# Recurrent gates as three products of high and low parts, low parts prepared early, and a tile's steps joined, in a two-layer hybrid flow step on one core

## The chip, the cores and the metric

The kernel runs on one core of one Trainium2 chip. The metric is device microseconds (us) of one execution. The time of the kernel before is 1498.38 us, the median of 3 runs (1497.87 to 1498.54). Engines are named as in the profile: PE is TensorE's products, PEld its weight loads, DVE VectorE, ACT ScalarE, POOL GpSimd and SP SyncE, which issues transfers.

## The reference

Two layers on 640 tokens (512 latents, 128 context) of width 1024, all in float32. Layer 0 mixes tokens by neighbourhood attention, layer 1 by a bidirectional gated linear recurrent unit; each is followed by a SwiGLU feed-forward. Every sub-layer has a norm, a shift and scale computed from the conditioning vector ("modulations"), and a gated residual. What the change touches is the recurrent unit:

```
xc  = depthwise conv of width 4 (xm @ w_x)             # 1024 channels, 8 blocks of 128
r   = sigmoid(xc_block @ w_a_block + b_a)              # per direction
i   = sigmoid(xc_block @ w_i_block + b_i)              # per direction
a   = exp(-8 * r * softplus(-lam))
b   = sqrt(1 - a^2) * (i * xc)
h_t = a_t * h_(t-1) + b_t                              # forward and backward
y   = gelu(xm @ w_g) * (h_forward + h_backward)        # then y @ w_lo
```

## The kernel before

Activations lie transposed: 128 channels of a tile in the partitions, tokens along the free axis. A dense weight is cut into units of 128 output channels by 1024 input channels (512 KB). A unit is used as a high part in TensorE's faster f32 format (`whi`, type fp32r) and a low part, what the high part leaves of the full value (`wlo`). The activations are split in the same way (`big` high and low). A product of full accuracy is three products: high by high, high by low, low by high (L239 to L241). `unit` (L170 to L189) prepares a unit: the raw weight comes by an SP transfer, the high part by ACT or by a POOL transfer that casts on the way, and DVE subtracts one from the other for the low part (L188).

The work goes through one program order that a scheduler fills in; each engine's instructions run in the order in which they stand on it, and so do the transfers of each queue. The stages, by the profiled execution:

- attention, to about 311 us;
- the first feed-forward with the attention's output projection ("ffn0", to about 835 us): 22 inner tiles in three chunks, each tile with a gate and an up unit (`ws`), then the chunk's down projection. Beside it DVE computes the remaining modulations: each step of the generator `mods` loads a 512 KB piece (`mraw`) on POOL's queue and multiplies it with the conditioning vector (`mprod`, L263 to L269). `fill(n)` takes n steps at each weight unit, up to a quota of the phase;
- the recurrent stage (835 to 1003 us): 8 tiles f of 128 channels. For each tile there are two weight units: `lru_xr` (the input of the conv) and `lru_gate` (the gelu branch). Each has 24 products of 384 columns and 24 of 256. `lru_a` does the conv on DVE and ACT and then the gate products: 2 gates by 2 directions, 643 columns (512 latents, 3 zeros and 128 context tokens) in plain f32 with one 128 by 128 weight block each, as products of 512 and 131 columns (L1407). ACT takes their tanh from PSUM (`gp`, two buffers, L1408). `lru_b` makes the coefficients (two exponential curves, a root) on ACT and DVE, with activation table loads (L1386) between the kinds of curve; `lru_c` the scans and the sum of both directions on DVE; `lru_d` and `lru_end` the product with the gelu branch and the split into `yhi`, `ylo`. The loop runs KT + 2 = 10 rounds: round t does `lru_a` of tile t, the input unit of tile t + 1, `lru_b` of tile t - 1, and `lru_c`, the gelu unit and `lru_d` of tile t - 2;
- the projection `project_halves` with w_lo (from about 980 us): 75 products over the first five input tiles of five outputs, then the later tiles as they become ready (L1093, L1097);
- the second feed-forward, to 1495 us, of which nothing is changed.

Of the kernel before, what the change touches and what calls it, by code (L numbers as in the profile page):

```python
# [15 lines left out]
P = 128  # L16
D = 1024
# [16 lines left out]
VW = 256  # L34
LW = 643
NLT = 10
C0 = 515
LATPR = (slice(0, 512), slice(C0, LW))
FG = (1, 1, 1)
MODS = ((0, 2), (0, 4), (0, 3), (0, 5), (1, 1), (1, 0), (1, 4), (1, 3), (1, 2), (1, 5))  # L40
# [87 lines left out]
class _Step:  # L128
# [40 lines left out]

    def unit(self, src, slot=None, after=None, nx=3, cast=False, raw=None):  # L170
        nc = self.nc
        _, a, b = src.shape
        raw = self.raw(src) if raw is None else raw
        if slot is None:
            self.nu += 1
            slot = "x" if self.wx and self.nu % 2 == 0 else "m"
        if slot == "x":
            hi, lo = self.wxs([P, a, b], nx)
        else:
            hi = self.t([P, a, b], F32R, "whi", 3)  # L180
            lo = self.t([P, a, b], F32R, "wlo", 3)
        if cast or self.ptags == ["at"]:
            with self.pin(self.cast if after else None):
                nc.gpsimd.dma_start(hi, src)
        else:
            nc.scalar.copy(hi, raw)  # L186
        with self.pin(after):
            self.low = nc.vector.tensor_tensor(lo, raw, hi.bitcast(F32), ALU.subtract).ins  # L188
        return hi, lo  # L189
# [70 lines left out]
    def mod_cols(self, l, j, out):  # L260
        nc = self.nc
        for f in range(KT):
            w = self.t([P, D], F32, "mraw", 2, self.sb)  # L263
            nc.gpsimd.dma_start(w, self.i["wm"][l * 6 + j - 2, f])  # L264
            for s in range(2):
                prod = self.t([P, D], F32, "mprod", 1, self.sb)
                with self.tc.issue_after(self.anchor) if self.anchor else nullcontext():
                    nc.vector.scalar_tensor_tensor(prod, w, 1.0, self.csb[:, s], ALU.mult, ALU.mult, accum_out=out[:, s, f:f + 1])  # L268
            yield  # L269
        nc.vector.tensor_tensor(out, out, self.col(f"bm{l}{j}").unsqueeze(1).broadcast_to([P, 2, KT]), ALU.add)  # L270
# [15 lines left out]
    def modulations(self):  # L286
        yield from self.mod_gate(0, 2)
        yield from self.mod_ss(0, 3, 1)
        yield from self.mod_gate(0, 5)
        yield from self.mod_ss(1, 0, 0)  # L290
        yield from self.mod_ss(1, 3, 1)
        yield from self.mod_gate(1, 2)
        yield from self.mod_gate(1, 5)

    def fill(self, n):
# [698 lines left out]
    def ffn(self, l, hi, lo, fp, last):  # L994
        nc = self.nc
        f0 = 0
        for ci, n in enumerate((8, 7, 7)):
# [23 lines left out]
            for j in range(n):  # L1021
                f = f0 + j
                self.ws(self.i["gu"][l, f], hi, lo, eg(j), FG[0] * (f > 0), CHB)
                self.ws(self.i["gu"][l, NF + f], hi, lo, eu(j), FG[1] * (f > 0), CHB)
            w = self.i["dn"][l, :, :, f0:f0 + n]
            if ci == 2:
                last(w, hhi, hlo, (l, 5))
            else:
                self.project(w, hhi, hlo, (l, 5), done=lambda f: self.fill(FG[2]))
            f0 += n  # L1030
# [334 lines left out]

    def halves(self, w, hi, lo, ev, after=None, slot=None):
        u = self.unit(w, slot, after, 2)
        return [lambda t0=t0, t1=t1, **kw: ev(t0, self.chunk(u, hi, lo, t0, t1, **kw)) for t0, t1 in CHL]

    def lru_xr(self, f, hi, lo, after=None):  # L1370
        xr = self.xrs[f % 2]
        nat = xr[:, 2:514].rearrange("p (r c) -> p c r", r=ROWS)

        def ev(t0, ps):
            for o, a, b, r in ((nat[:, 56:64], 0, 64, ROWS), (nat[:, 0:40], 64, 384, ROWS),
                               (nat[:, 40:56], 384, 512, ROWS), (xr[:, 517:645], 512, 640, 0)):
# [3 lines left out]
        return self.halves(self.i["wi"][KT + f], hi, lo, ev, after)  # L1380

# [8 lines left out]
    def lru_a(self, f, lp):  # L1390
        nc, xr = self.nc, self.xrs[f % 2]
        gw = self.t([P, 2, 2, P], F32, "gw", 2, lp)
        nc.sync.dma_start(gw, self.i["wg"][f])
        xc = self.t([P, LW], F32, "xc", 2, lp)
        nc.scalar.activation(xc, xr[:, 0:LW], AF.Identity, scale=self.col("cw0", f), bias=self.col("cb", f))
        for j in range(1, 4):
            nc.vector.scalar_tensor_tensor(xc, xr[:, j:j + LW], self.col(f"cw{j}", f), xc, ALU.mult, ALU.add)

        def lt():
            return self.t([P, 2, LW], F32, "lt", NLT, lp)  # L1400
        tr, ti = lt(), lt()
        for w, tl in enumerate((tr, ti)):
            for d in range(2):
                c = (w * 2 + d) * KT + f
                ps = self.pp.tile([P, 1024], F32, tag="gp", name=self.nm("gp"), bufs=2)
                for s0, s1 in ((0, 512), (512, LW)):
                    nc.tensor.matmul(ps[:, s0:s1], gw[:, w, d], xc[:, s0:s1], start=True, stop=True)  # L1407
                self.turn(AF.Exp, lambda: nc.scalar.activation(tl[:, d], ps[:, 0:LW], AF.Tanh, scale=0.5, bias=self.hb[:, c:c + 1]))  # L1408
        nc.vector.scalar_tensor_tensor(ti, ti, 1.0, xc[:, None, :].broadcast_to([P, 2, LW]), ALU.add, ALU.mult)
# [29 lines left out]
    def states(self, f, h):  # L1439
        ends = bass.AP(tensor=h.tensor, offset=h[:, 0, LW - 1:LW].offset, ap=[list(h.ap[0]), [C0 + 1, 2]])  # L1440
        return self.nc.vector.tensor_copy(self.st.rearrange("p (d k) -> p k d", d=2)[:, f], ends)

    def lru_c(self, f, a, h):
# [5 lines left out]
        for piece in ((56, 64, 0), (0, 56, 64)):  # L1449
            self.directions(y, h, *piece)  # L1450
        self.nc.vector.tensor_tensor(y[:, NLAT:NTOK], h[:, 0, C0:LW], h[:, 1, C0:LW], ALU.add)
        return y
# [12 lines left out]
    def lru_end(self, f, a, h, root, G, yhi, ylo, late):  # L1465
# [30 lines left out]
        dve(self.directions, y, h, 32, 56, 320)  # L1496
        dve(nc.vector.tensor_tensor, y[:, NLAT:NTOK], h[:, 0, C0:LW], h[:, 1, C0:LW], ALU.add)
        gated(*CH[1])
# [11 lines left out]
    def lru_gate(self, f, hi, lo, lp, after=None):  # L1510
# [3 lines left out]
        def ev(t0, ps):  # L1514
# [4 lines left out]
            for v, o in ((G, G),) if f == KT - 1 else ((ps, G[:, t0:NTOK]), (G[:, 0:t0], G[:, 0:t0])):  # L1519
                self.turn(AF.Gelu_apprx_tanh, lambda: nc.scalar.activation(o, v, AF.Gelu_apprx_tanh))  # L1520
        return G, self.halves(self.i["wi"][f], hi, lo, ev, after)

# [8 lines left out]
    def run(self):  # L1531
# [13 lines left out]
        self.cs = self.t([P, 2 * KT], F32, "cs", 1)  # L1545
        dram = self.ctx.enter_context(tc.tile_pool(name="dram", bufs=1, space=bass.MemoryType.DRAM))
        mpool, xpool = ExitStack(), ExitStack()
# [14 lines left out]
        V = V.rearrange("p k t -> p (k t)")[:, 0:NT * D].rearrange("p (t d) -> p t d", t=NT)  # L1562
        O = self.big(F32)
        with self.phase("attn", tp=2, sp=2, op=1, quota=24) as ap:
            self.kz = [self.t([P, 2, 960], F32R, f"KZ{j}", 1, ap) for j in range(2)]
# [32 lines left out]
        xd = dram.tile([D, NTOK], F32, tag="xd", name="xd")  # L1598
        with self.phase("ffn0", at=2, rr=1, mx=2, wx=2, quota=56) as fp:
# [5 lines left out]
            self.ffn(0, xhi, xlo, fp, last)  # L1605
        xpool.close()
        mpool.close()
# [5 lines left out]
        with self.phase("lru", at=1) as lp:  # L1613
            A, B, C, G = {}, {}, {}, {}
            self.table, self.last_act = AF.Gelu_apprx_tanh, None
# [66 lines left out]
```

## Time and profile before

| what | us |
|---|---|
| median of 3 runs | 1498.38 (1497.87 to 1498.54) |
| the profiled execution | 1496.74 |
| its span, from the first to the last instruction | 1494.9 |
| PE busy | 1475.9 (99%) |
| DVE busy | 1062.0 (71%) |
| ACT busy | 698.6 (47%) |
| POOL busy | 225.7 (15%) |
| granted TensorE clock, mean | 0.998 |

The profile is one execution on the hardware. A timeline row gives start, duration, engine, line, operation, the buffers written and read, the shape and the count; in square brackets the idle time of the engine just before, and what ended it. A row of a group gives busy time, the mean in ns of one instruction, and the idle time before them with what ended it. A transfer's row gives its queue, count, size and the median time from issue to landing. Successive products overlap on TensorE, so the duration of a product is longer than the distance to the next start.

### The profile page before, as it was taken

To read this page: it belongs to the slowest core of one execution; us is meant where nothing else is said; L and a number is where in the kernel's file an instruction comes from. 1 tells how busy PE (TensorE), PEld (TensorE's weight loads), DVE (VectorE), ACT (ScalarE), POOL (GpSimd) and SP (SyncE) were. 2 spreads that over 40 slices of the span, in tenths; PEclk is the share of its full clock that TensorE was granted. 3 is DMA by queue.
4 is the path that set the end of the run, shared out by engine and by line. 5 is a ranking of instruction groups with operands and counts; after the bars stand their busy time and mean duration, and the time that the engine had idled before them with its cause. 6 is when DMAs were issued, how large, how long until landed. Compare 5 with 4: busy or idle time off the path is not lost. (4 is left out here: it accounts for less than half of the span.)

```text
span 1494.9 us, 26171 instructions
## 1 busy us (share of the span) xinstructions
PE 1475.9 (99%) x10399; PEld 1433.0 (96%) x10399; DVE 1062.0 (71%) x2019; ACT 698.6 (47%) x1269; POOL 225.7 (15%) x264
## 2 busy tenths in 40 slices
PE   9999999999999999999999999999999999999997
PEld 7999999899999999999999988899999999999997
DVE  5778998679999987444443769886975666655645
ACT  5676667754332123312321569875634343424243
POOL 0212132101111110000000100000331322232311
PEclk9999999999999999999999999999999999999999
DMA  9645665345566664222222444335333131313111
GB/s 378 201 128 177 196 189 163 105 156 183 196 187 195 207 197 142 63 85 85 66 62 96 142 145 126 115 115 194 102 130 98 57 114 57 113 57 111 59 57 71
DMA packets 73050, 198.88 MB, mean 133 GB/s; under 512 B 8128, under 2 KB 24672, under 8 KB 72800
## 3 DMA queue, kind: packets, MB, share of 16 engines
q1 hardware_dynamic: 57360, 142.31, 29.9%
q0 software_dynamic: 14960, 54.21, 11.8%
q8 instruction: 82, 1.34, 0.4%
q10 hardware_dynamic: 608, 0.69, 0.1%
q14 instruction: 40, 0.33, 0.1%
HBM read 181.05 MB, written 8.92 MB: 127 GB/s over the span
## 5 line engine op out<-in xcount | busy, mean ns | idle before, releaser
L240 PE MATMUL mm<-big,whi 128*128 128x320 f32 (+3 forms) x1193 | 371.2, 311 | 0.8 <-DVE big L1508 0.6
L239 PE MATMUL mm<-big,whi 128*128 128x320 f32 (+3 forms) x1193 | 369.0, 311 | 1.6 <-ACT big L615 0.6
L241 PE MATMUL mm<-big,wlo 128*128 128x320 f32 (+3 forms) x1193 | 368.8, 310 | 0.0
L239 PEld LDWEIGHTS mm<-big,whi 128*128 128x128 f32 x1193 | 223.9, 188 | 3.7 <-ACT big L615 0.9
L240 PEld LDWEIGHTS mm<-big,whi 128*128 128x128 f32 x1193 | 224.2, 188 | 2.8 <-DVE big L1508 1.0
L241 PEld LDWEIGHTS mm<-big,wlo 128*128 128x128 f32 x1193 | 224.7, 188 | 1.1
L268 DVE SCALAR_TENSOR_TENSOR mprod<-mraw,csb 128x1024 f32<-128x1024 f32 x160 | 194.8, 1218 | 11.3 <-DMA mraw<-in_wm 10.8
L639 DVE SCALAR_TENSOR_TENSOR x<-mm,G,x 128x128 f32<-128x128 f32 (+3 forms) x193 | 77.4, 433 | 78.5 <-PE mm L241 77.0
L186 ACT CAST whi<-raw 128x1024 fp32r<-128x1024 f32 (+1 forms) x70 | 72.8, 1040 | 106.1 <-PE mm L240 71.2
L188 DVE TENSOR_TENSOR wlo<-raw,whi 128x1024 fp32r<-128x1024 f32 (+1 forms) x87 | 105.1, 1208 | 23.9 <-ACT whi L186 11.0
L240 PE MATMUL mm<-big,whx 128*128 128x320 f32 (+3 forms) x363 | 112.2, 309 | 0.0
L241 PE MATMUL mm<-big,wlx 128*128 128x320 f32 (+3 forms) x363 | 112.1, 309 | 0.0
L239 PE MATMUL mm<-big,whx 128*128 128x320 f32 (+3 forms) x363 | 111.9, 308 | 0.0
L264 POOL DMA_DIRECT2D mraw<-in_wm x80 | 43.4, 543 | 355.5 <-DVE mprod L268 257.3
L240 PE MATMUL mx<-big,whi 128*128 128x320 f32 (+3 forms) x299 | 92.1, 308 | 0.0
L239 PE MATMUL mx<-big,whi 128*128 128x320 f32 (+3 forms) x299 | 91.9, 307 | 0.0
L241 PE MATMUL mx<-big,wlo 128*128 128x320 f32 (+3 forms) x299 | 91.8, 307 | 0.0
L186 ACT CAST whx<-raw 128x1024 fp32r<-128x1024 f32 (+1 forms) x38 | 39.1, 1028 | 94.1 <-PE mm L240 54.5
L1506 ACT CAST whi<-raw 128x1024 fp32r<-128x1024 f32 (+1 forms) x41 | 41.3, 1007 | 69.0 <-PE mm L240 43.0
L240 PE MATMUL mx<-big,whx 128*128 128x320 f32 (+3 forms) x234 | 72.9, 312 | 0.0
L241 PE MATMUL mx<-big,wlx 128*128 128x320 f32 (+3 forms) x234 | 72.6, 310 | 0.0
L239 PE MATMUL mx<-big,whx 128*128 128x320 f32 (+3 forms) x234 | 72.4, 309 | 0.0
(409 smaller groups left out, 3734.3 us busy)
## 6 DMA issues: line engine op xcount, KB each, us to landing
raw<-in_gu SPq DMA_DIRECT2D x88, 512.0 KB, 3.5
mraw<-in_wm POOLq DMA_DIRECT2D x80, 512.0 KB, 3.9
raw<-in_dn SPq DMA_DIRECT2D x24, 512.0 KB, 3.6
sw<-in_wm SPq DMA_DIRECT2D x16, 512.0 KB, 10.2
raw<-in_wqk SPq DMA_DIRECT2D x16, 512.0 KB, 4.9
raw<-in_wi SPq DMA_DIRECT2D x16, 512.0 KB, 3.5
whi<-in_wi POOLq DMA_DIRECT2D x16, 512.0 KB, 3.8
raw<-in_dn SPq DMA_DIRECT2D x16, 448.0 KB, 3.3
```

Of the source, the lines that this page charges most:

```text
L186: nc.scalar.copy(hi, raw)
L188: self.low = nc.vector.tensor_tensor(lo, raw, hi.bitcast(F32), ALU.subtract).ins
L239: nc.tensor.matmul(ps, hi[:, k], xhi[:, k, s], start=(k == 0), stop=False)
L240: nc.tensor.matmul(ps, hi[:, k], xlo[:, k, s], start=False, stop=False)
L241: self.done = nc.tensor.matmul(ps, lo[:, k], xhi[:, k, s], start=False, stop=(k == last)).ins
L264: nc.gpsimd.dma_start(w, self.i["wm"][l * 6 + j - 2, f])
L268: nc.vector.scalar_tensor_tensor(prod, w, 1.0, self.csb[:, s], ALU.mult, ALU.mult, accum_out=out[:, s, f:f + 1])
L639: self.added = self.nc.vector.scalar_tensor_tensor(xs, ps[:, a - t0:b - t0], G[:, s, f:f + 1], xs, ALU.mult, ALU.add).ins
L1506: self.nc.scalar.copy(hi, v)
```

## The change

Three things are changed together.

1. The gate products. The row of 643 columns is made 644 long (LW; LE keeps the true length). `xc` is split into `xh` (ACT) and `xl` (DVE); the gate weights come as a high part (`gw`, cast by a POOL transfer) and a low part (`gx`, loaded by SP). Each gate and direction is three products of two pieces of 322 columns, each piece in its own PSUM bank, and the tanh reads both banks.
2. The low parts of the recurrent stage's weights. The 16 units and the 8 gate weight blocks are prepared in ffn0 by a generator that follows the modulations (`lows`): per weight two POOL transfers in (one casting), one DVE subtract, one POOL transfer to DRAM. In the recurrent stage SP loads the low part straight into its place, and the raw load and the DVE subtract there are gone. The steps at the weight units of the second chunk become two (FG), the quota 81, and `mprod` gets a second buffer in this phase.
3. The rounds. `lru_b` of tile t runs in the same round as `lru_a` of tile t, and `lru_c`, the gelu unit and `lru_d` are those of tile t - 1: KT + 1 = 9 rounds. In round 7 the gelu units of the tiles 6 and 7 both stand there.

```
-LW = 643
+LW = 644
+LE = 643
-LATPR = (slice(0, 512), slice(C0, LW))
-FG = (1, 1, 1)
+LATPR = (slice(0, 512), slice(C0, LE))
+FG = (1, 2, 1)
...
-    def unit(self, src, slot=None, after=None, nx=3, cast=False, raw=None):
+    def unit(self, src, slot=None, after=None, nx=3, cast=False, raw=None, low=None):
...
+        if low is not None:
+            nc.sync.dma_start(lo.bitcast(F32), low)
+            return hi, lo
...
+        yield from self.lows()
+
+    def lows(self):
+        nc = self.nc
+        held = None
+        for key, src in self.split_ahead + [(None, None)]:
+            if key is not None:
+                shape = list(src.shape)
+                raw = self.t(shape, F32R, "mraw", 2, self.sb)
+                hi = self.t(shape, F32R, "mprod", 2, self.sb)
+                nc.gpsimd.dma_start(hi, src)
+                nc.gpsimd.dma_start(raw.bitcast(F32), src)
+            if held:
+                k, r, h = held
+                with self.pin(self.done):
+                    nc.vector.tensor_tensor(r, r.bitcast(F32), h.bitcast(F32), ALU.subtract)
+                self.low_parts[k] = self.dram.tile(list(r.shape), F32, tag=f"low{k[0]}{k[1]}", name=f"low{k[0]}{k[1]}")
+                nc.gpsimd.dma_start(self.low_parts[k], r.bitcast(F32))
+            held = key and (key, raw, hi)
+            yield
...
-    def halves(self, w, hi, lo, ev, after=None, slot=None):
-        u = self.unit(w, slot, after, 2)
+    def halves(self, k, hi, lo, ev, after=None):
+        u = self.unit(self.i["wi"][k], None, after, 2, low=self.low_parts["i", k])
...
-        gw = self.t([P, 2, 2, P], F32, "gw", 2, lp)
-        nc.sync.dma_start(gw, self.i["wg"][f])
+        gw, gl = [self.t([P, 2, 2, P], F32R, v, 2, lp) for v in ("gw", "gx")]
+        nc.gpsimd.dma_start(gw, self.i["wg"][f])
+        nc.sync.dma_start(gl.bitcast(F32), self.low_parts["g", f])
...
+        xh, xl = [self.t([P, D], F32R, "raw", 3)[:, 0:LW] for j in range(2)]
+        self.split(xh, xl, xc)
...
-                for s0, s1 in ((0, 512), (512, LW)):
-                    nc.tensor.matmul(ps[:, s0:s1], gw[:, w, d], xc[:, s0:s1], start=True, stop=True)
-                self.turn(AF.Exp, lambda: nc.scalar.activation(tl[:, d], ps[:, 0:LW], AF.Tanh, scale=0.5, bias=self.hb[:, c:c + 1]))
+                gs = ps.rearrange("p (b c) -> p b c", b=2)[:, :, 0:LW // 2]
+                for v, x in ((gw, xh), (gl, xh), (gw, xl)):
+                    for b in range(2):
+                        nc.tensor.matmul(gs[:, b], v[:, w, d], x[:, b * LW // 2:(b + 1) * LW // 2], start=(x is xh and v is gw), stop=(x is xl))
+                o = tl[:, d].rearrange("p (b c) -> p b c", b=2)
+                self.turn(AF.Exp, lambda: nc.scalar.activation(o, gs, AF.Tanh, scale=0.5, bias=self.hb[:, c:c + 1]))
...
-            for t in range(KT + 2):
+            for t in range(KT + 1):
                 if t < KT:
-                    A[t] = self.lru_a(t, lp)
+                    ab = self.lru_a(t, lp)
                 if t + 1 < KT:
                     for step in self.lru_xr(t + 1, xhi, xlo) if t else x1[1:]:
                         step()
-                if 0 < t <= KT:
-                    B[t - 1] = self.lru_b(t - 1, *A.pop(t - 1))
-                if t > KT:
-                    ended = self.lru_end(t - 2, *B.pop(t - 2), G.pop(t - 2), yhi, ylo, late)
-                elif t > 1:
-                    C[t - 2] = self.lru_c(t - 2, *B.pop(t - 2))
-                for g in {KT - 1: (KT - 3, KT - 2), KT: (KT - 1,)}.get(t, (t - 2,)):
-                    for step in gate(g) if 0 < g < KT - 1 + (t == KT) else ():
+                if t < KT:
+                    B[t] = self.lru_b(t, *ab)
+                if t == KT:
+                    ended = self.lru_end(t - 1, *B.pop(t - 1), G.pop(t - 1), yhi, ylo, late)
+                elif t > 0:
+                    C[t - 1] = self.lru_c(t - 1, *B.pop(t - 1))
+                for g in (t - 1, t) if t == KT - 1 else (t - 1,):
+                    for step in gate(g) if 0 < g and t < KT else ():
                         step()
-                if 1 < t <= KT:
-                    late = self.lru_d(t - 2, C.pop(t - 2), G.pop(t - 2), yhi, ylo)
+                if 0 < t < KT:
+                    late = self.lru_d(t - 1, C.pop(t - 1), G.pop(t - 1), yhi, ylo)
```

In the listings of the order, lines are 25 to 35 higher after the change than before (L239 to L241 are L244 to L246, L188 is L193, L616 is L641, L1407 is L1437, L1408 is L1439).

More of the change, by code (lines that the diff above doesn't have):

```diff
@@ L168, in raw @@
         return t
-    def unit(self, src, slot=None, after=None, nx=3, cast=False, raw=None):
+    def unit(self, src, slot=None, after=None, nx=3, cast=False, raw=None, low=None):
         nc = self.nc
         _, a, b = src.shape
-        raw = self.raw(src) if raw is None else raw
+        if low is None:
+            raw = self.raw(src) if raw is None else raw
         if slot is None:
@@ L265, in mod_cols @@
             for s in range(2):
-                prod = self.t([P, D], F32, "mprod", 1, self.sb)
+                prod = self.t([P, D], F32, "mprod", self.mb, self.sb)
                 with self.tc.issue_after(self.anchor) if self.anchor else nullcontext():
@@ L1022, in ffn @@
                 f = f0 + j
-                self.ws(self.i["gu"][l, f], hi, lo, eg(j), FG[0] * (f > 0), CHB)
-                self.ws(self.i["gu"][l, NF + f], hi, lo, eu(j), FG[1] * (f > 0), CHB)
+                self.ws(self.i["gu"][l, f], hi, lo, eg(j), FG[ci == 1] * (f > 0), CHB)
+                self.ws(self.i["gu"][l, NF + f], hi, lo, eu(j), FG[ci == 1] * (f > 0), CHB)
             w = self.i["dn"][l, :, :, f0:f0 + n]
@@ L1028, in ffn @@
             else:
-                self.project(w, hhi, hlo, (l, 5), done=lambda f: self.fill(FG[2]))
+                self.project(w, hhi, hlo, (l, 5), done=lambda f: self.fill(FG[f0 > 0]))
             f0 += n
@@ L1379, in ev @@
                     self.nc.scalar.copy(o, v.rearrange("p (c r) -> p c r", r=r) if r else v)
-        return self.halves(self.i["wi"][KT + f], hi, lo, ev, after)
+        return self.halves(KT + f, hi, lo, ev, after)
     def turn(self, table, step):
@@ L1439, in states @@
     def states(self, f, h):
-        ends = bass.AP(tensor=h.tensor, offset=h[:, 0, LW - 1:LW].offset, ap=[list(h.ap[0]), [C0 + 1, 2]])
+        ends = bass.AP(tensor=h.tensor, offset=h[:, 0, LE - 1:LE].offset, ap=[list(h.ap[0]), [LW + C0 - LE + 1, 2]])
         return self.nc.vector.tensor_copy(self.st.rearrange("p (d k) -> p k d", d=2)[:, f], ends)
@@ L1450, in lru_c @@
             self.directions(y, h, *piece)
-        self.nc.vector.tensor_tensor(y[:, NLAT:NTOK], h[:, 0, C0:LW], h[:, 1, C0:LW], ALU.add)
+        self.nc.vector.tensor_tensor(y[:, NLAT:NTOK], h[:, 0, C0:LE], h[:, 1, C0:LE], ALU.add)
         return y
@@ L1496, in lru_end @@
         dve(self.directions, y, h, 32, 56, 320)
-        dve(nc.vector.tensor_tensor, y[:, NLAT:NTOK], h[:, 0, C0:LW], h[:, 1, C0:LW], ALU.add)
+        dve(nc.vector.tensor_tensor, y[:, NLAT:NTOK], h[:, 0, C0:LE], h[:, 1, C0:LE], ALU.add)
         gated(*CH[1])
@@ L1520, in ev @@
                 self.turn(AF.Gelu_apprx_tanh, lambda: nc.scalar.activation(o, v, AF.Gelu_apprx_tanh))
-        return G, self.halves(self.i["wi"][f], hi, lo, ev, after)
+        return G, self.halves(f, hi, lo, ev, after)
     def new_x(self, st):
@@ L1545, in run @@
         self.cs = self.t([P, 2 * KT], F32, "cs", 1)
-        dram = self.ctx.enter_context(tc.tile_pool(name="dram", bufs=1, space=bass.MemoryType.DRAM))
+        self.dram = dram = self.ctx.enter_context(tc.tile_pool(name="dram", bufs=1, space=bass.MemoryType.DRAM))
+        self.low_parts = {}
+        order = [KT, 0, KT + 1] + [k for f in range(1, KT) for k in ((f, KT + f + 1) if f + 1 < KT else (f,))]
+        self.split_ahead = [(("i", k), i["wi"][k]) for k in order] + [(("g", f), i["wg"][f]) for f in range(KT)]
         mpool, xpool = ExitStack(), ExitStack()
@@ L1563, in run @@
         O = self.big(F32)
+        self.mb = 1
         with self.phase("attn", tp=2, sp=2, op=1, quota=24) as ap:
@@ L1598, in run @@
         xd = dram.tile([D, NTOK], F32, tag="xd", name="xd")
-        with self.phase("ffn0", at=2, rr=1, mx=2, wx=2, quota=56) as fp:
+        self.mb = 2
+        with self.phase("ffn0", at=2, rr=1, mx=2, wx=2, quota=81) as fp:
             self.project(i["wo"], ohi, olo, (0, 2), ((0, 1), xhi, xlo), None, True)
@@ L1605, in run @@
             self.ffn(0, xhi, xlo, fp, last)
+            assert next(self.mods, None) is None
         xpool.close()
@@ L1613, in run @@
         with self.phase("lru", at=1) as lp:
-            A, B, C, G = {}, {}, {}, {}
+            B, C, G = {}, {}, {}
             self.table, self.last_act = AF.Gelu_apprx_tanh, None
```

## Prediction

> **What bounds the kernel now.** I read the page's busy shares and clock first, then the windows by stage, then TensorE's timeline for the few places where it stands still.
>
> ```profile
> PE 1475.9 (99%) x10399; PEld 1433.0 (96%) x10399; DVE 1062.0 (71%) x2019; ACT 698.6 (47%) x1269; POOL 225.7 (15%) x264
> PEclk9999999999999999999999999999999999999999
> ```
>
> ```profile
> 600.00:835.00 235.00, 235.00 (x1607) 235.00 (x1606) 103.51 (x189) 61.91 (x116) 2.52 (x4) 1.00 0.27 81
> 862.00:980.00 118.00, 117.94 (x697) 102.40 (x696) 99.88 (x120) 95.61 (x130) 5.29 (x10) 1.00 0.41 122
> ```
>
> A window row gives start and end, length, busy time of PE, weight loads, DVE, ACT and POOL, granted clock, DMA share, GB/s. PE is full in the first feed-forward (here 600 to 835) and in the middle of the recurrent stage (862 to 980), at full clock. So the time is the number of TensorE products by their spacing, plus the few gaps. A record's duration (0.31 us) is not its price, because products overlap: the price is the distance from one start to the next. The gaps that this change can reach lie at the two ends of the recurrent stage:
>
> ```profile
> 836.11 0.49 PE L592 MATMUL at<-ones,ssq 128*128 128x128 f32 x2 [0.66 <-DVE ssq L578]
> ...
> 838.58 0.34 PE L241 MATMUL mm<-big,wlo 128*128 128x384 f32 x1
> 839.47 0.44 PE L239 MATMUL mm<-big,whi 128*128 128x384 f32 x1 [0.56 <-ACT big L615]
> 840.12 0.44 PE L240 MATMUL mm<-big,whi 128*128 128x384 f32 x1 [0.21 <-DVE big L616]
> ...
> 999.75 0.31 PE L1093 MATMUL mx<-big,whi 128*128 128x320 f32 x1
> ...
> 1000.19 0.31 PE L1093 MATMUL mx<-big,wlo 128*128 128x320 f32 x1
> 1002.00 0.41 PE L1093 MATMUL mm<-big,whi 128*128 128x320 f32 x1 [1.50 <-ACT big L1481]
> ```
>
> **Part 1, the gate products.** There are 8 tiles by 2 gates by 2 directions, 32 products of 643 columns, each issued as 512 and 131 columns in full f32.
>
> ```profile
> 872.21 1.24 PE L1407 MATMUL gp<-xc,gw 128*128 128x512 f32 x4
> 873.21 0.42 PE L239 MATMUL mm<-big,whi 128*128 128x384 f32 x1
> 873.46 0.33 PE L240 MATMUL mm<-big,whi 128*128 128x384 f32 x1
> 873.63 0.34 PE L241 MATMUL mm<-big,wlo 128*128 128x384 f32 x1
> ```
>
> One takes 873.21 - 872.21 = 1.00 us, and the product behind it is 0.08 late (0.25 to its successor, where 0.17 is usual): 1.08 each, 34.6 us in all. Now each becomes six products of 322 columns. Layer 0 has such products already:
>
> ```profile
> 378.39 0.30 PE L239 MATMUL mm<-big,whx 128*128 128x322 f32 x1
> ...
> 379.87 0.31 PE L240 MATMUL mm<-big,whx 128*128 128x322 f32 x1
> ...
> 381.14 0.31 PE L241 MATMUL mm<-big,wlx 128*128 128x322 f32 x1
> ...
> 382.49 0.31 PE L241 MATMUL mm<-big,wlx 128*128 128x322 f32 x1
> ```
>
> Ten spacings make 1.48 us in the first piece, nine 1.35 in the second: 0.149 each, so 0.894 for six, 0.187 less than now, 32 times **-6.0 us**. All of it is on the path, PE being full.
>
> ```order
> L241 MATMUL mm_10776<-big_8919,wlo_10747 128x256
> L1407 MATMUL gp_10655<-xc_10639,gw_10637 128x512
> L1407 MATMUL gp_10655<-xc_10639,gw_10637 128x131
> L1407 MATMUL gp_10659<-xc_10639,gw_10637 128x512
> L1407 MATMUL gp_10659<-xc_10639,gw_10637 128x131
> L239 MATMUL mm_10831<-big_8919,whi_10827 128x384
> ```
>
> Above is PE at the last gate of the last tile before (mm_10831 is that tile's other weight unit, lru_gate), below the same place after:
>
> ```order
> L246 MATMUL mm_11170<-big_9087,wlo_11141 128x256
> L1437 MATMUL gp_11046<-raw_11023,gw_11014 128x322 x2
> L1437 MATMUL gp_11046<-raw_11023,gx_11015 128x322 x2
> L1437 MATMUL gp_11046<-raw_11024,gw_11014 128x322 x2
> L1437 MATMUL gp_11054<-raw_11023,gw_11014 128x322 x2
> L1437 MATMUL gp_11054<-raw_11023,gx_11015 128x322 x2
> L1437 MATMUL gp_11054<-raw_11024,gw_11014 128x322 x2
> L244 MATMUL mm_11252<-big_9699,whi_11236 128x320
> ```
>
> The six products stand there in place of the pair, and the unit of 48 products has moved ahead of the gate: behind it the next layer product (mm_11252) comes at once.
>
> The Trainium skill, "TensorE: Matmul & The Clock Gate", section "Wait — 56ns, not 53.3ns?", puts a warm product's spacing at N / 2.4 GHz plus about 2.5 ns: an estimate of 0.137 us at 322 columns, which would save about 8.3 us instead of 6.0. By it the sum would be 2.3 lower; the trace's 0.149 disagrees, and the trace decides.
>
> **Part 2, the stage's start.** DVE is without a break there, and its chain feeds PE at 839.47:
>
> ```profile
> 835.97 1.21 DVE L188 TENSOR_TENSOR wlo<-raw,whi 128x1024 fp32r<-128x1024 f32 x1
> 837.11 1.14 DVE L616 SCALAR_TENSOR_TENSOR big<-nv,B,big 128x384 fp32r<-128x384 f32 x2
> 838.16 0.60 DVE L614 SCALAR_TENSOR_TENSOR nv<-x,A,rr 128x384 f32<-128x384 f32 x1
> ```
>
> ```order
> L616 SCALAR_TENSOR_TENSOR big_8920<-nv_9350,B_1108_6023,big_8919 128x384
> L578 TENSOR_TENSOR ssq_8950<-ssq_8950,sq_9414 128x256
> L188 TENSOR_TENSOR wlo_9560<-raw_9557,whi_9559 128x1024
> L616 SCALAR_TENSOR_TENSOR big_8920<-nv_9382,B_1108_6023,big_8919 128x384
> L616 SCALAR_TENSOR_TENSOR big_8920<-nv_9386,B_1108_6023,big_8919 128x384
> ```
>
> That is DVE's list at this place before; after, the subtract is out of it (big is the normed input, high and low part):
>
> ```order
> L641 SCALAR_TENSOR_TENSOR big_9088<-nv_9518,B_1108_6023,big_9087 128x384
> L641 SCALAR_TENSOR_TENSOR big_9088<-nv_9550,B_1108_6023,big_9087 128x384
> L664 SCALAR_TENSOR_TENSOR x_4130<-mx_9586,G_680_3223,x_4130 128x128 x2
> L641 SCALAR_TENSOR_TENSOR big_9088<-nv_9554,B_1108_6023,big_9087 128x384
> L603 TENSOR_TENSOR ssq_9118<-ssq_9118,sq_9582 128x256
> ```
>
> With 1.21 us out of the chain the PE gaps at 839.47 (0.72 beyond the usual spacing) and 840.12 (0.48) should close: **-1.2 us**. If the wait is really for the residual sums that feed the norm, nothing goes; if the gap at 836.11 (0.82) closes too, 2.0. The low part now comes from DRAM by SP. A unit's load takes about 3.5 us (Part 5) against 7.0 us of products in a unit (24 spacings of 0.175 and 24 of 0.12, next rows), so it lies under them; what SP queues behind such a load are stores of x, which nobody reads until after the stage.
>
> ```profile
> 976.25 0.28 PE L240 MATMUL mm<-big,whi 128*128 128x256 f32 x1
> ...
> 976.49 2.33 PE L1407 MATMUL gp<-xc,gw 128*128 128x512 f32 x8
> 978.57 0.42 PE L239 MATMUL mm<-big,whi 128*128 128x384 f32 x1
> ```
>
> **Part 3, the joined steps.** A tile's second half now runs in the same round as its gates. Groups of ACT, then of DVE, in the stage (850 to 1005):
>
> ```profile
> L1386 ACT ACT_TABLE_LOAD x22 | 28.2, 1283 | 0.4
> L1408 ACT ACTIVATE lt<-gp,l_hb 128x643 f32<-128x643 f32 x32 | 24.9, 797 | 19.6 <-PE gp L1407 19.4
> L1506 ACT CAST big<-lt 128x640 fp32r<-128x640 f32 x5 | 3.7, 738 | 0.4 <-DVE lt L1455 0.4
> L1520 ACT ACTIVATE gl<-gl 128x384 f32<-128x384 f32 x7 | 3.6, 517 | 0.0
> ```
>
> ```profile
> L188 DVE TENSOR_TENSOR wlo<-raw,whi 128x1024 fp32r<-128x1024 f32 x15 | 18.4, 1224 | 11.5 <-DMA whi<-in_wi 5.0 <-issue 4.6 <-PE gp L1407 1.9
> L1508 DVE TENSOR_TENSOR big<-lt,big 128x640 fp32r<-128x640 f32 x5 | 4.1, 826 | 0.0
> ```
>
> The cast costs about 0.74 us (as L1506). A tile takes PE two units, 14.1, and four gate products: 18.4 us before, 17.6 now. ACT was busy 95.61 of 118, or 14.9 a tile, now 15.6: 2.0 us stay free. New meeting points remain: gate products that wait for PSUM until the tanh before them is through (0.80), a unit that waits for a gelu (0.52). If each binds at a few tiles, 0 to 2.5 us; I take **+1.1**, one wait of each at about 0.55. DVE loses two subtracts a tile (2.4, L188) and gains the xl subtract (0.83, as L1508); xl waits for ACT's cast with the next tile's chain queued behind it, and has 1.6 us in hand.
>
> **Part 4, the stage's end.** Before, the last tile's coefficients were ready behind 48 + 100 products (from 978.57 to 1000.19), and PE still waited 1.67. Now only 90 products of 0.147 (13.2 us) lie between the last gate and the first product that needs the last but one tile (spacing from the rows 999.75 to 1000.19), whose gated sum stands on DVE behind the last tile's scans. On ACT the last tile's whole curve (lt_11063 is a, lt_11027 the tanh of r, then the root) comes after its last tanh:
>
> ```order
> L1439 ACTIVATE lt_11028<-gp_11046,l_hb_2038 128x644
> L1439 ACTIVATE lt_11028<-gp_11054,l_hb_2038 128x644
> L1449 ACTIVATE lt_11063<-lt_11027,l_sm_392_2036 128x644 x2
> L1453 ACTIVATE lt_11027<-lt_11027,l_sp_391_2034 128x644 x2
> L1411 ACT_TABLE_LOAD
> L1454 ACTIVATE lt_11027<-lt_11027 128x1288
> ```
>
> Before, the exponentials of the tile ahead (lt_10475) stood there, and its own came after them:
>
> ```order
> L1408 ACTIVATE lt_10645<-gp_10655,l_hb_2038 128x643
> L1408 ACTIVATE lt_10645<-gp_10659,l_hb_2038 128x643
> L1418 ACTIVATE lt_10664<-lt_10475,l_sm_392_2036 128x643 x2
> L1422 ACTIVATE lt_10475<-lt_10475,l_sp_391_2034 128x643 x2
> L1386 ACT_TABLE_LOAD
> ```
>
> So the last tile's own curve has moved to stand directly behind its last tanh, and nothing of another tile is ahead of it. The lengths, from ACT's timeline before and then DVE's and the cast by DMA:
>
> ```profile
> 989.99 1.75 ACT L1418 ACTIVATE lt<-lt,l_sm 128x643 f32<-128x643 f32 x2
> ...
> 994.95 1.28 ACT L1423 ACTIVATE lt<-lt 128x1286 f32<-128x1286 f32 x1
> ```
>
> ```profile
> 996.26 1.23 DVE L1473 TENSOR_TENSOR lt<-lt,lt 128x1024 f32<-128x1024 f32 x1 [0.41 <-ACT lt L1423]
> 997.52 2.46 DVE L1432 TENSOR_TENSOR_SCAN lt<-lt,cols,lt 128x512 f32<-128x512 f32 x2
> ```
>
> ```profile
> big<-lt POOLq DMA_DIRECT2D x2, 320.0 KB, 2.6
> ```
>
> The chain: 0.8 (tanh), 6.2 (989.99 to the end of the root), 3.7 (to the scans' end, 996.26 to 999.98), 0.8 for the gated sum (as L1508) and 2.6 for its cast by DMA, some 0.6 between: 14.7 against 13.2, a gap of 1.5 in place of 1.67: **0**, between -1.7 (cover holds) and +4.5.
>
> **Part 5, the low parts in the first feed-forward.** 24 subtracts (16 of 1.2, 8 of half the size at about half that: 24 us) and 72 transfers on POOL's queue:
>
> ```profile
> raw<-in_wi SPq DMA_DIRECT2D x16, 512.0 KB, 3.5
> mraw<-in_wm POOLq DMA_DIRECT2D x80, 512.0 KB, 3.9
> L268 DVE SCALAR_TENSOR_TENSOR mprod<-mraw,csb 128x1024 f32<-128x1024 f32 x160 | 194.8, 1218 | 11.3 <-DMA mraw<-in_wm 10.8
> ```
>
> They come after the modulation steps, about where DVE is 44% busy (103.51 of 235) and DMA 27%. The subtract waits for a load of 3.9 us issued a step earlier, and a step is 7 us of products: **0**, unless loads come late; then residual sums queue behind the waiting subtract on DVE, and PE waits for their PSUM. On POOL each store waits for its subtract, and the next step's loads stand behind it.
>
> **Sum.** -6.0 - 1.2 + 1.1 + 0 + 0 = -6.1 on the profiled execution (1494.9 span, 1496.74 in all): 1490.6. That execution lies 1.64 under the median 1498.38, so 1492.3 against the median. 0.2%, 3.0 us, is about what a measurement here can tell from no change.
>
> **Rivals.** *ACT becomes the pace* (slower). Row L1408 waits 19.4 us for gate products, 2.4 a tile. Inside one round the loop of gate, tanh, exponentials, cast, next gate is closed; busy 15.6 plus a wait of 2.4 makes 18.0, and with another 0.9 a tile (a table load of 1.28 that nothing covers would do) the round is 18.9, 1.3 longer than PE's 17.6, over 8 tiles 10.4: 1502.7. It is slower by 3.0 from (3.0 + 6.1) / 8 = 1.14 a tile on. Against it: today's waits are ACT being early, and shrink as it falls behind. *The tail eats it*: +4.5 in Part 4, if the first subtract of a wlo unit or the POOL queue stands ahead: 1496.8, no measurable change. *The low parts disturb the first feed-forward*: 24 steps each holding PE 0.25 us are 6 us: 1498.3. For it speaks the order of DVE, which doesn't pass a waiting subtract. The Trainium skill, "SBUF — State Buffer", section "SBUF: two separate sides", warns that transfers issued by GpSimd starve while DVE holds the shared port; the trace shows 3.9 us on POOL beside 3.5 on SP, with DVE nearly full, so little of it. *The products don't do what they say*: if the change from one kind to the other costs 0.08 at each product as now, 32 times 0.08 or 2.6 is lost: 1494.9. *Closer products*: 0.137 would give another 192 times 0.012, 2.3 less: 1490.0; but 0.149 at 322 columns, 0.147 at 320 and 0.175 at 384 are all 0.46 ns a column.
>
> **Chances.** Forecast 0.65, closer products 0.02, weaker products 0.04, tail 0.13 (of it 0.03 still faster), low parts 0.06, ACT 0.10. So faster 0.74, same 0.16, slower 0.10. Range: down to 1488.0 (6.0 + 2.0 + 1.7 gained, and 0.7 if the products come at 0.145), up to 1499.0, which leaves out most of the ACT case alone.
>
> **What would show it.** Right: six gp products spaced 0.149; PE gaps at 839 and 840 gone; one gap of 1 to 2 us before the last products of the wlo projection; no PE gap from 600 to 835. Wrong: PE waiting at gp for ACT in most tiles, or a stage that isn't some 6 us shorter.

## The result and the profile after

The changed kernel takes 1505.61 us (median of 4 runs, 1504.28 to 1506.31) against 1498.12 before (4 runs, 1497.21 to 1498.54): ratio 1.0051, 95% interval 1.0039 to 1.0064. It is slower by 7.5 us; 1492.3 was forecast. The profiled execution took 1504.28, its span is 1502.5 (before 1494.9).

The windows of the first feed-forward show it at once. First the page's busy line, then two windows after (start:end, length, busy time of PE, weight loads, DVE, ACT, POOL, granted clock, DMA share, GB/s), and the first of them before:

```profile
PE 1474.3 (98%) x10463; PEld 1446.4 (96%) x10463; DVE 1068.4 (71%) x2035; ACT 702.4 (47%) x1277; POOL 271.4 (18%) x344
```

```profile
368.00:600.00 232.00, 228.67 (x1553) 228.50 (x1552) 204.36 (x376) 63.67 (x119) 37.38 (x65) 0.99 0.67 216
600.00:835.00 235.00, 229.61 (x1531) 229.35 (x1530) 113.42 (x191) 58.49 (x112) 30.38 (x57) 0.99 0.50 166
```

```profile
368.00:600.00 232.00, 232.00 (x1585) 232.00 (x1583) 205.95 (x378) 66.49 (x124) 27.90 (x50) 1.00 0.58 183
```

PE was full in both stretches before, with 1585 and 1607 products; now 1553 and 1531 fit into them. To place the loss, take two products that both kernels have: the one of the closing projection's norm (836.11 before, in the prediction's rows) and the first of the second feed-forward's norm. Before, then after:

```profile
1049.12 0.38 PE L592 MATMUL at<-ones,ssq 128*128 128x128 f32 x2
```

```profile
848.75 0.38 PE L617 MATMUL at<-ones,ssq 128*128 128x128 f32 x2
...
1057.38 0.38 PE L617 MATMUL at<-ones,ssq 128*128 128x128 f32 x2
```

Up to the first mark the changed kernel loses 848.75 - 836.11 = 12.6 us. Between the marks, the recurrent stage and its projection, it takes 208.6 us instead of 213.0: 4.4 gained. Behind the second mark the spans leave 445.1 against 445.8. So the recurrent stage gained 4.4 us of the 6.1 that were forecast, and the loss of 12.6 us lies ahead of it, where the prediction had put nothing.

There PE stands still twice. Its timeline around the first stall:

```profile
381.68 0.83 PE L634 MATMUL rr<-dg,ones 128*128 128x128 f32 x6
385.85 0.91 PE L634 MATMUL rr<-dg,ones 128*128 128x128 f32 x6 [3.33 <-DVE dg L626]
386.51 0.39 PE L244 MATMUL mx<-big,whx 128*128 128x320 f32 x1
...
387.03 0.46 PE L244 MATMUL mx<-big,whx 128*128 128x320 f32 x1
387.29 0.47 PE L245 MATMUL mx<-big,whx 128*128 128x320 f32 x1
...
390.22 0.41 PE L244 MATMUL mx<-big,whx 128*128 128x320 f32 x1
390.47 0.31 PE L245 MATMUL mx<-big,whx 128*128 128x320 f32 x1
390.62 0.31 PE L246 MATMUL mx<-big,wlx 128*128 128x320 f32 x1
```

And around the second, at the end of the second chunk:

```profile
645.49 0.30 PE L244 MATMUL mx<-big,whi 128*128 128x320 f32 x1
651.19 0.64 PE L245 MATMUL mm<-big,whx 128*128 128x320 f32 x1 [5.39 <-DVE big L1539]
651.62 0.47 PE L246 MATMUL mm<-big,wlx 128*128 128x320 f32 x1
651.88 0.47 PE L245 MATMUL mx<-big,whi 128*128 128x320 f32 x1
652.15 0.47 PE L246 MATMUL mx<-big,wlo 128*128 128x320 f32 x1
```

Each costs twice. First the wait: 3.50 and 5.55 us beyond the usual spacing. Then products of 320 columns come at 0.267 us instead of 0.147 for some microseconds, 1.6 us more behind the first stall and 2.6 behind the second. The windows show why (the column ahead of the last two is the granted clock): it is halved.

```profile
387.00:390.00 3.00, 3.00 (x14) 3.00 (x13) 3.00 (x7) 1.24 (x4) 0.52 (x1) 0.50 0.62 246
391.00:395.00 4.00, 4.00 (x29) 4.00 (x28) 2.57 (x5) 1.05 (x1) 0.00 (x0) 1.00 0.36 125
652.00:656.00 4.00, 4.00 (x17) 4.00 (x16) 2.62 (x6) 0.80 (x1) 1.70 (x4) 0.50 0.78 222
657.00:661.00 4.00, 4.00 (x30) 4.00 (x29) 1.46 (x3) 0.95 (x1) 0.54 (x1) 1.00 1.06 410
```

Together 3.50 + 1.6 + 5.55 + 2.6 = 13.3 us; a stall of 0.82 ahead of 836.11 is gone, which leaves 12.4, and the work ahead of the first stall is 0.4 longer in this execution: 12.8, about the 12.6. (Both kernels have equally many products up to the first mark. Compared place by place in PE's order, the changed one is 0.4 us late ahead of the first stall and 5.5 behind it, 5.3 ahead of the second and 13.5 behind it.)

The trace says what the second stall waits for. DVE's timeline there, the issue of the load that it waits for on POOL, and the loads and stores of the low parts (median time from issue to landing):

```profile
642.44 1.08 DVE L193 TENSOR_TENSOR wlo<-raw,whi 128x896 fp32r<-128x896 f32 x1
649.51 1.23 DVE L314 TENSOR_TENSOR mraw<-mraw,mprod 128x1024 fp32r<-128x1024 f32 x1 [5.98 <-DMA mraw<-in_wi]
650.65 0.48 DVE L1539 TENSOR_TENSOR big<-sg,big 128x320 fp32r<-128x320 f32 x1
```

```profile
643.83 0.54 POOL L310 DMA_DIRECT2D mraw<-in_wi  x1 [3.90 <-DMA lowi<-mraw]
```

```profile
mraw<-in_wi POOLq DMA_DIRECT2D x16, 512.0 KB, 7.3
mprod<-in_wi POOLq DMA_DIRECT2D x16, 512.0 KB, 6.4
lowi<-mraw POOLq DMA_DIRECT2D x16, 512.0 KB, 5.0
```

DVE waits 5.98 us for a low part's load, and the last hidden tile's low part (big, L1539), for which PE waits, stands behind it. The load is late because POOL issues it at 643.83 only, when the store of an earlier low part has landed and its buffer is free, and because it then takes more than 5 us.

### The profile page after: what moved, and what is told of

It is laid out like the page before. It is cut to its first block, busy times and chain, and to the rows that moved or that the text cites. A ratio compares the mean times of both kernels' runs of the same rounds, so it can differ in the third digit from the quotient of the medians.

```text
span 1502.5 us, 26459 instructions
## 1 busy us (share of the span) xinstructions
PE 1474.3 (98%) x10463; PEld 1446.4 (96%) x10463; DVE 1068.4 (71%) x2035; ACT 702.4 (47%) x1277; POOL 271.4 (18%) x344
## 5 line engine op out<-in xcount | busy, mean ns | idle before, releaser
L244 PE MATMUL mm<-big,whi 128*128 128x320 f32 (+3 forms) x1193 | 368.1, 310 | 2.3 <-ACT gl L1551 1.6
L246 PE MATMUL mm<-big,wlo 128*128 128x320 f32 (+3 forms) x1193 | 368.9, 310 | 0.0
L244 PEld LDWEIGHTS mm<-big,whi 128*128 128x128 f32 x1193 | 224.2, 188 | 4.5 <-ACT gl L1551 2.1
L246 PEld LDWEIGHTS mm<-big,wlo 128*128 128x128 f32 x1193 | 224.8, 189 | 1.1
L188 ACT CAST whi<-raw 128x1024 fp32r<-128x1024 f32 (+1 forms) x70 | 72.9, 1042 | 102.7 <-PE mm L245 66.2
L246 PE MATMUL mm<-big,wlx 128*128 128x320 f32 (+3 forms) x363 | 112.3, 309 | 0.0
L244 PE MATMUL mm<-big,whx 128*128 128x320 f32 (+3 forms) x363 | 111.9, 308 | 0.0
L193 DVE TENSOR_TENSOR wlo<-raw,whi 128x1024 fp32r<-128x1024 f32 (+1 forms) x71 | 85.6, 1206 | 13.2 <-ACT whi L188 13.2
L246 PE MATMUL mx<-big,wlo 128*128 128x320 f32 (+3 forms) x299 | 92.6, 310 | 0.0
L244 PE MATMUL mx<-big,whi 128*128 128x320 f32 (+3 forms) x299 | 92.6, 310 | 0.0
L188 ACT CAST whx<-raw 128x1024 fp32r<-128x1024 f32 (+1 forms) x38 | 39.1, 1028 | 104.8 <-PE mm L245 64.8
L245 PEld LDWEIGHTS mm<-big,whx 128*128 128x128 f32 x363 | 68.4, 188 | 5.7 <-DVE big L1539 5.7
L246 PE MATMUL mx<-big,wlx 128*128 128x320 f32 (+3 forms) x234 | 73.3, 313 | 0.0
L244 PE MATMUL mx<-big,whx 128*128 128x320 f32 (+3 forms) x234 | 73.2, 313 | 0.0
```

The source lines that it names most:

```text
L244: nc.tensor.matmul(ps, hi[:, k], xhi[:, k, s], start=(k == 0), stop=False)
L245: nc.tensor.matmul(ps, hi[:, k], xlo[:, k, s], start=False, stop=False)
L246: self.done = nc.tensor.matmul(ps, lo[:, k], xhi[:, k, s], start=False, stop=(k == last)).ins
```

## The experiments

The theory after the trace: the loss is the two stalls and their half-rate tails; the first comes from the second product buffer of the modulation steps, the second from where the low parts' subtracts stand in DVE's order. Rivals: the new gates or the joined rounds hold up the recurrent stage; or low parts beside the feed-forward cost time wherever they stand. Each ratio is against the kernel before, run on the same chip.

**Gates alone.** The low parts of the units and of the gate weights are made by DVE in the recurrent stage, rounds and steps as before. Part of the edit, against the changed kernel:

```
-        u = self.unit(self.i["wi"][k], None, after, 2, low=self.low_parts["i", k])
+        u = self.unit(self.i["wi"][k], None, after, 2)
...
-        gw, gl = [self.t([P, 2, 2, P], F32R, v, 2, lp) for v in ("gw", "gx")]
+        gw, gl = [self.t([P, 2, 2, P], F32R, v, b, lp) for v, b in (("gw", 2), ("gx", 1))]
...
-        nc.sync.dma_start(gl.bitcast(F32), self.low_parts["g", f])
...
+        nc.sync.dma_start(gr, self.i["wg"][f])
+        nc.vector.tensor_tensor(gl, gr, gw.bitcast(F32), ALU.subtract)
...
-        xh, xl = [self.t([P, D], F32R, "raw", 3)[:, 0:LW] for j in range(2)]
+        xh, xl = [self.t([P, LW], F32R, v, 1, lp) for v in ("xh", "xl")]
```

So this form also has one buffer each for `gx`, `xh` and `xl`, where the changed kernel has two for `gx` and takes the other two from the three of `raw`.

> Only the gate products are changed (three products of 322 columns); the low parts are made by a DVE subtract in the recurrent stage, rounds and the first feed-forward as before. Theory (the 7.5 us of the loss come from two TensorE stalls in the first feed-forward, each followed by products at half rate): no stall there, the gates' 6.0 us are gained: about 1492 against 1498.1. Rival (the new gates hold up the recurrent stage): 1496 or more.

Measured: 1504.20, ratio 1.0044 (1.0029 to 1.0059). The rival's number. The two longest of the waits of PE there:

```profile
942.71 0.39 PE L244 MATMUL mm<-big,whi 128*128 128x256 f32 x1 [2.18 <-ACT xr L1403]
...
1008.51 0.62 PE L1117 MATMUL mm<-big,whi 128*128 128x320 f32 x1 [3.43 <-ACT big L1513]
```

There is no stall in the first feed-forward, but from 836.89 to 1057.18, the same two marks, it takes 220.3 us against 213.0. With a cast, a subtract for xl and one for the gate weights added, and the units' subtracts still there, the chain over ACT and DVE no longer keeps up. So in this form the gates need the early low parts: in the recurrent stage the three edits are not separate terms. What the single buffers cost is not separated from it: DVE waits 4.0 us, in two places, for gate products before it may write `gx` again.

**Gates and joined rounds,** the low parts still made in the stage; the edit is the last one with the nine rounds kept.

> Gates and joined rounds, without the low parts prepared early, modulation steps with one product buffer and one step per unit as before. Theory: the rounds are worth within 1.5 us of nothing: 1490.5 to 1493.5. Rival (ACT becomes the pace once the rounds are joined): 1498 or more, with TensorE waiting at the gate products in most tiles.

Measured: 1501.47, ratio 1.0025 (1.0015 to 1.0034), 218.0 us between the marks. The rounds win 2.7 us over the run before, more than expected. The time is in the rival's range, but not by the rival's sign: the largest wait of PE is for a gelu, not at the gate products:

```profile
934.71 0.58 PE L244 MATMUL mm<-big,whi 128*128 128x256 f32 x1 [3.50 <-ACT gl L1552]
```

**The same with two product buffers.** One edit, `self.mb = 2` in the first feed-forward.

> As the run with gates and joined rounds, with one edit: the modulation steps' product tile has two buffers in the first feed-forward. Theory: that alone moves the norm's sums 60 places later on TensorE, the first stall (3.5 us) and 1.6 us of half-rate products behind it come back: 5 us above that run, about 1497. Rival (the first stall belongs to the low parts or their transfers): no difference.

Measured: 1508.03, ratio 1.0062 (1.0045 to 1.0078), 6.6 us above the run without it, where 5 were expected. The first stall is back with no low part in the kernel:

```profile
385.75 1.62 PE L633 MATMUL rr<-dg,ones 128*128 128x128 f32 x6 [3.33 <-DVE dg L625]
```

So that stall belongs to the second buffer. Before, other products stand between the two groups of rr, and PE waits at neither:

```profile
375.67 0.83 PE L609 MATMUL rr<-dg,ones 128*128 128x128 f32 x6
...
380.03 0.83 PE L609 MATMUL rr<-dg,ones 128*128 128x128 f32 x6
```

With two buffers, PE has the sums of the norm (at) 60 places later in its order, 21 places ahead of the first spreading product (rr) instead of 43, and the second one directly behind the first instead of 26 places: PE has run out of other products before DVE has worked out the scale (dg).

**One low part per unit.** The steps at a weight unit are held to one while units' low parts are due, up to three for the small ones.

```
     def fill(self, n):
+        n = self.lowphase or n
```

> The changed kernel with one low part of a unit per weight unit instead of two in the second chunk (the eight small ones up to three per unit). Theory: the loads land in time, the second stall (5.6 us) and its 2.5 us of half-rate products go: 8 us less than the changed kernel, about 1497.5, with the first stall still there. Rival (the transfers are late at any rate, by contention): about 1505.

Measured: 1503.66, ratio 1.0041 (1.0026 to 1.0056). The second stall stays, 5.30 us at 645.43. The theory's first form falls: how many steps a unit takes in the program does not set when the subtracts run.

**One product buffer** in the changed kernel (the low parts keep two under two names).

> The changed kernel with one product buffer for the modulation steps, as before the change (the low parts keep two, the second under a name of its own). Theory: the first stall (3.5 us, at the norm of the first feed-forward) and its 1.6 us of half-rate products go, all else stays: 5 us less than the changed kernel, about 1500.5. Rival (the first stall comes from elsewhere): 1505.

Measured: 1497.97 (1493.32 to 1501.85 over 10 runs), ratio 0.9998 (0.9986 to 1.0010). The first stall is gone, as in every run with one buffer; the second is there, and the times spread over 8.5 us, where those of the kernel before spread over 3. That the second stall varies from one execution to the next is inferred from this spread, one execution of each kernel being traced. In this one, of 1500.10 us:

```profile
644.84 0.64 PE L244 MATMUL mm<-big,whx 128*128 128x320 f32 x1 [6.21 <-ACT big L1538]
```

**No steps at the chunk's end,** alone and together with one product buffer:

```
-                self.ws(self.i["gu"][l, f], hi, lo, eg(j), FG[ci == 1] * (f > 0), CHB)
...
+                fg = (f > 0, 2 * (j < 5), 2)[ci] if l == 0 else FG[ci == 1] * (f > 0)
+                self.ws(self.i["gu"][l, f], hi, lo, eg(j), fg, CHB)
...
-                self.project(w, hhi, hlo, (l, 5), done=lambda f: self.fill(FG[f0 > 0]))
+                self.project(w, hhi, hlo, (l, 5), done=lambda f: self.fill(FG[f0 > 0] * (f > 0 or f0 == 0)))
```

> The changed kernel without steps at the last two tiles of the second chunk and at the first tile of its down projection; what is left over moves to the third chunk, two a unit. Theory: DVE's late subtract costs TensorE time only where the chunk's last hidden tile is awaited, so the second stall (5.6 us) and its 2.3 us of half-rate products go: 7.9 us less, about 1497.7. Rival (late loads cost wherever the steps lie): the stall moves into the third chunk or to its end, 1503 or more.

> Both edits of the two runs before this one together. Theory: the whole loss was these two stalls with their half-rate tails (13 us): about 1492.4, faster than the kernel before by 5 to 6 us. Rival (the recurrent stage itself lost time): 1496 or more.

Measured: 1504.60, ratio 1.0047 (1.0031 to 1.0064), and 1499.21 (1493.79 to 1503.50), ratio 1.0006 (0.9993 to 1.0019). Both miss, with times in the rivals' ranges but not for the rivals' reasons: the stall did not move, and the recurrent stage lost nothing (208.4 and 208.6 us between the marks). The second stall is still at the end of the second chunk (3.23 us at 646.93, 2.48 at 638.83 in the profiled ones). The steps at that place were never the ones that ran there. Counted through the program, the first low part belongs to the down projection behind the second chunk, which PE begins at about 645; its subtract ran at 566.4 in the changed kernel. The pin on it, `self.pin(self.done)`, names a product on PE, and DVE's order is not held by it. So low parts run one after another as fast as their buffers allow, some 80 us ahead of their place, between the swiglu steps of the second chunk.

**Ten rounds** in the changed kernel.

> The changed kernel with the ten rounds of before. Theory: with the low parts off DVE the joined rounds are worth 0 to 3 us: 1505.5 to 1508.5. Rival (joining costs time in the recurrent stage): below 1504.

Measured: 1507.49, ratio 1.0063 (1.0048 to 1.0078), as expected. Between the marks 210.2 us against 208.6: the joined rounds are worth 1.6 us where the low parts are early.

**One load per low part.** ACT casts the high part, DVE writes the low part over it, so that the raw buffer is free at once; one product buffer.

```
-                nc.gpsimd.dma_start(hi, src)
-                nc.gpsimd.dma_start(raw.bitcast(F32), src)
+                nc.gpsimd.dma_start(raw, src)
...
+                    nc.scalar.copy(h, r)
+                nc.vector.tensor_tensor(h, r, h.bitcast(F32), ALU.subtract)
```

> The changed kernel with one product buffer for the modulations, and the low parts prepared with one load in place of two: the high part is cast by ACT, DVE writes the low part over the high one, so that the next load waits for no store; one unit's low part per step. Theory (the second stall comes from a buffer's cycle of subtract, store, load, 13 us for two buffers): no stall in the first feed-forward, about 1491.5 to 1493. Rival (any low parts beside the feed-forward hold up DVE there): a stall of 3 us or more stays at the second chunk's end, 1496 or more.

> As the run before this one, but with the gate products of before (full f32, 512 and 131 columns, no split of xc, no low parts of the gate weights). Theory (the gates are worth what their spacing says): 5 to 6 us above that run, about 1497.5. Rival (in the joined rounds the gates' saving is lost in waits): within 2 us of it.

Measured: 1498.28, ratio 1.0003 (0.9994 to 1.0012), and with f32 gates 1500.24 (1495.85 to 1502.64), ratio 1.0016 (1.0007 to 1.0025). The low parts come every 4.3 us on the average instead of 6.5, and the stall at the chunk's end stays (3.61 us), as the rival expected:

```profile
642.76 0.41 PE L244 MATMUL mm<-big,whx 128*128 128x320 f32 x1 [3.61 <-ACT big L1540]
```

A faster buffer cycle does not cure it. The second of the pair says little on the gates by its median, since its times spread over 6.8 us; between the marks it takes 209.6 us against 208.3.

**Low parts ordered late.** The last edit with the pins on instructions of the same engine, then the same with f32 gates:

```
-                with self.pin(self.done):
+                with self.pin(self.cast_at):
                     nc.scalar.copy(h, r)
+                with self.pin(self.sub_at):
+                    nc.vector.tensor_tensor(h, r, h.bitcast(F32), ALU.subtract)
```

(cast_at and sub_at are the last hidden tile's cast on ACT and split on DVE, or the last residual sum.)

> As the run with one load per low part, but each low part's cast and subtract are kept, on their own engines, behind the last tile's swiglu or residual sum of their place in the program (the changed kernel ties them to a TensorE product, and DVE's order still has them some 60 us ahead of it). Theory (the second stall is a matter of where the subtracts stand in DVE's order, ahead of work that TensorE waits for): no stall at the second chunk's end, 7 us less than that run: about 1491.5, and a spread of the times no wider than before. Rival (low parts in the first feed-forward cost time wherever they stand): 1496 or more.

> As the run before this one with the f32 gates of before. By the stage of the earlier pair of runs the new gates are worth 1.3 us here, because part of their 6 us goes into waits for ACT and DVE: 1 to 2 us above that run, about 1493. Rival (they are worth their 6 us once nothing else stalls): about 1497.5.

Measured: 1491.39 (1490.60 to 1492.05 over 5 runs), ratio 0.9955 (0.9943 to 0.9968), and 1492.57 (1492.01 to 1493.76), ratio 0.9964 (0.9951 to 0.9978). Both are as the theory expected, and both beat the kernel before. The window of the first, with all low parts in it, has every product that it had before:

```profile
600.00:835.00 235.00, 235.00 (x1607) 235.00 (x1606) 126.98 (x215) 82.75 (x142) 27.21 (x50) 1.00 0.49 162
```

So the low parts cost nothing where they stand behind the urgent work of their engine: DVE's idle time ahead of the 24 subtracts falls from 35.4 us in the run with one load per low part to 5.3, the data being there when their turn comes. They now run from 659.4 to 783.2, between the second chunk's last hidden tile (636.2) and the third's (785.3), so this run doesn't show what a subtract ordered late at a chunk's end itself would cost. The rival of the recurrent stage falls for the whole change, and stands for the gates alone.

The pair also prices the gates in a kernel without other stalls: 1.2 us by the medians (0.8 between the marks, 208.9 against 209.7, and 1.3 in the earlier pair), not 6.0. With f32 gates PE has no wait above 0.44 us from the first mark to the end of the projection; with the new ones it has four, 1.13 and 0.73 for a gelu on ACT, 1.60 and 1.42 at the tail for the cast by DMA. ACT's rows at the tanh tell why, first with the new gates, then with f32 gates:

```profile
L1445 ACT ACTIVATE lt<-gp,l_hb 128x644 f32<-128x644 f32 x32 | 24.6, 798 | 6.1 <-PE gp L1443 5.5
```

```profile
L1439 ACT ACTIVATE lt<-gp,l_hb 128x643 f32<-128x643 f32 x32 | 24.8, 797 | 13.6 <-PE gp L1438 13.5
```

ACT had 13.5 us of slack ahead of the tanh; the new gates use 8.0 of it, and PE begins to wait for ACT. The eight casts of `xh` are 5.9 us of work on ACT that the f32 gates don't have. That the two waits at the tail have the same cause is argued, not shown.

## Why the prediction was wrong

**Part 1 (gates, -6.0): the size was right, the worth was not.** The rows of the changed kernel:

```profile
873.73 0.46 PE L1437 MATMUL gp<-raw,gw 128*128 128x322 f32 x2
...
875.50 0.34 PE L246 MATMUL mm<-big,wlo 128*128 128x384 f32 x1
```

Twelve products in 1.77 us are 0.885 for six, 0.894 was forecast (over all 32, 0.897). But that the whole saving lies on the path "PE being full" failed: shorter products and one more cast leave ACT less time, and 4.8 of the 6.0 come back as waits (the four above add up to 4.9).

**Part 2 (start, -1.2): right.** The stalls of 0.82, 0.72 and 0.48 are gone in the changed kernel, 2.0 in all: the upper bound. In the run with gates and joined rounds, where DVE still makes the low parts in the stage, they are there (0.75, 0.71 and 0.48).

**Parts 3 and 4 (+1.1 and 0): too low.** The waits came at the places named, for a gelu and at the tail, but there are two of each:

```profile
919.12 0.44 PE L244 MATMUL mm<-big,whi 128*128 128x384 f32 x1 [0.99 <-ACT gl L1551]
...
987.85 0.39 PE L244 MATMUL mm<-big,whi 128*128 128x256 f32 x1 [0.57 <-ACT gl L1551]
...
996.19 0.41 PE L1118 MATMUL mm<-big,whi 128*128 128x320 f32 x1 [0.99 <-DMA big<-lt]
...
1008.39 0.41 PE L1118 MATMUL mm<-big,whi 128*128 128x320 f32 x1 [1.25 <-DMA big<-lt]
```

Beyond the usual spacing they are 1.15, 0.73, 1.16 and 1.41. Against the tail of 1.67 before that is +2.8, where +1.1 was forecast. The two marks give -4.4 for the stage. On this the range would have held. These waits are the ones that eat the gates' saving, and not a loss beside it: in the run with the low parts ordered late and f32 gates none of them is there, and the old tail of 1.67 isn't either.

**Part 5 (low parts, 0): this step failed.** It said that the subtract waits for "a load of 3.9 us issued a step earlier, and a step is 7 us of products". Neither holds. The loads take 7.3 and 6.4 us and the store 5.0, and the steps are not spaced by products at all: the low parts run ahead, as fast as two buffers cycle. The mean DMA share, 27% before and 50% after, says little of the place: from 639.4 to 645.4, just ahead of the stall, the DMA engines are 92% busy. The prediction named the right mechanism as its condition (a late load, work behind a waiting subtract on DVE, though it thought of residual sums) and gave it 0.06 as a rival, priced at 24 small holds. It came as one stall at the one place where nothing covers DVE's delay, the chunk's last hidden tile: 5.55 us, and 2.6 of halved clock behind it.

**Missing altogether:** the second product buffer, named in the change and priced nowhere. It moved the norm's sums on PE: 3.50 and 1.6 us. The order of the program shows that move without any run; the prediction looked at the order in the recurrent stage alone. Why a buffer moves them was not asked.

**And a price missing in every term:** a stall of PE above some 2 us also costs clock.

The sum of 1492.3 is close to the run with the low parts ordered late (1491.39), which has the terms that were summed without the two stalls. This is in part luck. Between the marks the other two edits, with f32 gates, give 3.3 us (213.0 before, 209.7), where the sum had 0.1 for parts 2 to 4; the new gates add about 1 where it had 6.0.

## What to carry to other kernels

Read the order on every engine over the whole program when a buffer count or a helper's work changes, not only where the change aims: a second buffer for background work moved a norm by 60 places on another engine. Work put into an engine's idle time is free only if it stands behind what the busy engine waits for, on its own engine's order; a tie to another engine's instruction did not hold it. A mean share over 235 us does not show whether there is room at the place where the work will run. Where one engine is full, a saving on it is worth what the next engine's slack allows: look at how long that one waits for the first (here 13.5 us at the tanh), since the saving comes out of it.

## What the runs showed of the hardware

A stall of TensorE halves its granted clock, within the stall or behind it. In the profiles here stalls of 3.2 to 7.0 us were followed by products at about 0.267 us instead of 0.147 (320 columns) every time, for 3 to 6 us, 1.4 to 2.8 us more in all. So were stalls of 2.25 us (ten rounds), 2.34 (gates alone) and 2.48 (both edits together), with 11 to 17 slow products. Stalls of up to 1.7 us were followed by one or two slow products; one of 1.93 us was followed by 14 slow products in the run with gates and joined rounds, and by one in the run with two product buffers. The traces record the halved clock for 3.41 us at the first stall of the changed kernel, for 6.83 at the second, and for 10.24 in the run with one product buffer.

The Trainium skill, "TensorE: Matmul & The Clock Gate", section "Part 1: The HAM clock gate (the "warmup" mystery)", puts the drop at an idle window of about 3.4 us, and the return after about 3.4 us of work, with windows that run freely. The halved rate agrees (0.50 granted), and so do the stretches, multiples of 3.41 us; the stalls of 1.93 to 2.48 us that halved the clock were shorter than its figure.

Loads on POOL's queue took 6.4 and 7.3 us for 512 KB (medians) where each low part had two loads and a store, and 5.9 where it had one load and a store, against 3.9 and 4.0 for the modulations' loads in the same two runs. What of it comes from the stores and what from the other queues is not separated.
